# A batched 64x64 matmul: plain fp32 loads from GpSimd, and the cast to bf16 in one VectorE instruction

## The chip, the cores and the metric

The kernel runs on one core of a Trainium2 chip. The metric is the device time of one execution in microseconds (us); the time given for a kernel is the median of several executions. Engines are named as in the profile: PE is TensorE's matmul, PEld its weight load, DVE is VectorE, ACT is ScalarE, POOL is GpSimd and SP is SyncE, which here only issues transfers. Transfers can be issued from SP, ACT and POOL. All of them are carried out by the core's 16 DMA engines; in the profile the queue of POOL is q0, that of SP is q1 and that of ACT is q10.

## The reference

```python
a = randn(1024, 64, 64) as float32
b = randn(1024, 64, 64) as float32
out = matmul(a, b) as float32          # 1024 products of 64x64 by 64x64
```

Each of the three tensors has 16.78 MB (16 MiB).

## The kernel before

The batch is worked off in 16 tiles `t` of 64 matrices for `b` and the result, and in 8 tiles `s` of 128 matrices for `a`; tile `s` of `a` serves the tiles `t = 2s` and `t = 2s + 1`.

**Loading a.** A tile of `a` has 2 MiB and comes in four quarters `h` of 512 KiB. Each quarter is a 128-partition transfer with one contiguous row of 4 KB for each partition. For `s >= 1` (`load_a`, L69) POOL issues three quarters that are cast from fp32 to bf16 on the way, into `a_sb` (L73), and SP issues the fourth as plain fp32 into `a_raw` (L77). Both come from `a_pool`, which has three buffers of each. The first tile (`load_first_a`, L80) is loaded as plain fp32, two quarters from SP and two from ACT, into two buffers that are borrowed from the result pool `o_pool`, which has eight (L48).

**Loading b.** `load_b(t)` (L93) fetches 1 MiB of fp32 in pieces of 512 bytes, from SP for even `t` and from ACT for odd `t`, into one of three buffers. `cast(t)` (L144) turns it into bf16 on DVE, except the first tile, which ACT casts, and the last, which the two share (L149, L151).

**Regrouping and transposing a.** `regroup(s)` (L99) writes the quarters into `a_bf`, in which the four quarters lie side by side for each row `v`: one DVE copy of the three bf16 quarters (L108) and one DVE cast of the fp32 quarter (L111). For `s = 0` four casts do it, two on DVE and two on ACT (L105). `transpose(s, j)` reads pairs of bf16 as fp32 words and transposes them on PE (L120); ACT copies the result to `at_sb` (L123). `spread(t)` (L133) is four DVE copies that place the transposed words into a block-diagonal tile `at_bd`.

**Multiplying and storing.** `multiply(t)` runs 64 matmuls (L189) in two halves. The results are copied from PSUM into a result buffer `o_sb` (L177): eight copies of ACT for even tiles, six of ACT and two of DVE for odd ones, and a split into smaller ones for the last. `store(t)` (L166) writes the 1 MiB of a tile from POOL, one tile later than it was made (`HOLD = 2`); only the last two tiles are stored from SP and ACT, in pieces.

**The order.** The order of each engine's instructions and of each queue's transfers is that of the program, written out by hand:

```python
for t in range(n_t):
    ...
        spread(t + 1)
        cast(t + 1)
    ...
        load_b(t + B_AHEAD)
    ...
        load_a(s + 1 + A_AHEAD)
    ...
        transpose(s + 1, 1)
    multiply(t)
    ...
        regroup(s + 2)
    ...
        transpose(s + 2, 0)
        store(t - HOLD + 1)
```

The lines for `a` run once for each pair of tiles. An instruction waits for the semaphores of what it reads and of the buffer that it overwrites, and everything behind it on its engine waits with it; a transfer waits on the queue of the engine that issues it.

Of the kernel before, what the change touches and what calls it, by code (L numbers as in the profile page):

```python
# [8 lines left out]
fp32 = mybir.dt.float32  # L9
bf16 = mybir.dt.bfloat16  # L10
# [3 lines left out]
def kernel(  # L14
# [14 lines left out]
    nc = tc.nc  # L29
    B, M, K = a.shape  # L30
    _, _, N = b.shape
# [8 lines left out]
    a_v = a.rearrange("(s g h) (mp v) k -> s h g mp (v k)", h=4, g=32, v=16)  # L40
# [4 lines left out]
    a_pool = ctx.enter_context(tc.tile_pool(name="a_pool", bufs=A_AHEAD))  # L45
    b_pool = ctx.enter_context(tc.tile_pool(name="b_pool", bufs=B_AHEAD))
    work = ctx.enter_context(tc.tile_pool(name="work", bufs=2))
    o_pool = ctx.enter_context(tc.tile_pool(name="o_pool", bufs=8))  # L48
    t_psum = ctx.enter_context(
        tc.tile_pool(name="t_psum", bufs=4, space=bass.MemoryType.PSUM)  # L50
    )
# [9 lines left out]
    a_tiles, b_tiles, abf_tiles, at_tiles, bbf_tiles = {}, {}, {}, {}, {}  # L61
# [6 lines left out]

    def load_a(s):  # L69

        a_sb = a_pool.tile([128, 3, 16, 64], bf16, name="a_sb")
        for h in range(3):
            nc.gpsimd.dma_start(  # L73
                out=a_sb[:, h, :, :].rearrange("p v k -> p (v k)"), in_=a_v[s, h], single_packet=True
            )
        a_raw = a_pool.tile([128, 16, 64], fp32, name="a_raw")
        nc.sync.dma_start(out=a_raw[:].rearrange("p v k -> p (v k)"), in_=a_v[s, 3])  # L77
        a_tiles[s] = a_sb, a_raw

    def load_first_a():  # L80

        raw = [
            o_pool.tile([128, 8, 2, 2, 64], fp32, name="o_sb")[:].rearrange(
                "p gh j wl n -> p (gh j wl n)"
            )
            for _ in range(2)
        ]
        parts = [raw[h % 2][:, 1024 * (h // 2) : 1024 * (h // 2) + 1024] for h in range(4)]
        for h in range(4):
            (nc.scalar if h % 2 else nc.sync).dma_start(out=parts[h], in_=a_v[0, h])  # L90
        a_tiles[0] = parts

    def load_b(t):  # L93
        b_sb = b_pool.tile([128, 16, 128], fp32, name="b_sb")
        queue = nc.scalar if t % 2 else nc.sync
        queue.dma_start(out=b_sb[:], in_=b_v[t])  # L96
        b_tiles[t] = b_sb

    def regroup(s):  # L99
        a_sb = a_tiles.pop(s)  # L100
        a_bf = work.tile([128, 16, 4, 64], bf16, name="a_bf")
        if s == 0:
            for h in range(4):
                copy = nc.scalar.copy if h % 2 else nc.vector.tensor_copy
                copy(a_bf[:, :, h, :], a_sb[h].rearrange("p (v k) -> p v k", v=16))  # L105
        else:
            cast_sb, raw = a_sb
            nc.vector.tensor_copy(  # L108
                a_bf[:, :, 0:3, :], cast_sb[:].rearrange("p h v k -> p v h k")
            )  # L110
            nc.vector.tensor_copy(a_bf[:, :, 3, :], raw[:])  # L111
        abf_tiles[s] = a_bf
        at_tiles[s] = work.tile([128, 2, 32, 2, 4, 4], fp32, name="at_sb")

    def transpose(s, j):
        a_cols = abf_tiles[s][:].rearrange("p v h k -> p v (h k)").bitcast(fp32)
        for wl in range(2):
            at_ps = t_psum.tile([128, 4, 128], fp32, name="at_ps")
            for vo in range(4):
                nc.tensor.transpose(  # L120
                    at_ps[:, vo, :], a_cols[:, 4 * vo + 2 * j + wl, :], identity[:]
                )
            nc.scalar.copy(  # L123
                at_tiles[s][:, j, :, wl, :, :],
                at_ps[:].rearrange("p vo (g mp) -> p g mp vo", mp=4),
            )

    def spread(t):
        half = slice(16 * (t % 2), 16 * (t % 2) + 16)
        bd = bd_tiles[t % N_BD]  # L130
        for h in range(4):
            rows = slice(32 * h, 32 * h + 32)
            nc.vector.tensor_copy(  # L133
                bd[rows, :, :, :, h, :].rearrange("p j g wl mo -> p j (g wl) mo"),
                at_tiles[t // 2][rows, :, half, :, :, :].rearrange(
                    "p j g wl mp vo -> p j (g wl) (mp vo)"
                ),
            )

    def cast(t):  # L140
        b_bf = work.tile([128, 16, 128], bf16, name="b_bf")
        b_sb = b_tiles.pop(t)
        if t < n_t - 1:
            (nc.vector.tensor_copy if t else nc.scalar.copy)(b_bf[:], b_sb[:])  # L144
        else:
            for gq in range(4):
                rows = slice(4 * gq, 4 * gq + 4)
                if gq % 2:
                    nc.vector.tensor_copy(b_bf[:, rows, :], b_sb[:, rows, :])  # L149
                else:  # L150
                    nc.scalar.copy(b_bf[:, rows, :], b_sb[:, rows, :])  # L151
        bbf_tiles[t] = b_bf

    def store(t):
        for piece in held.pop(t):
            piece()
# [51 lines left out]
            held[t] = [lambda q=q: put(q, 8 if whole else 4) for q in ([0] if whole else [0, 4])]  # L208

    with tc.manual_schedule():  # L210
        load_first_a()

        nc.vector.memset(warm[:, 0:1], 0.0)
        nc.scalar.copy(warm[:, 1:2], warm[:, 0:1])  # L214
        load_b(0)
        load_b(1)
        nc.vector.memset(bd_tiles[0][:], 0.0)  # L217
        make_identity(nc, identity)
        nc.gpsimd.memset(bd_tiles[1][:, 0], 0.0)
        load_a(1)  # L220
        load_b(2)
        nc.gpsimd.memset(bd_tiles[1][:, 1], 0.0)
        load_a(2)
        regroup(0)
        transpose(0, 0)
        transpose(0, 1)
        spread(0)
        cast(0)
        for t in range(n_t):
            s, half = t // 2, t % 2  # L230
            if t + 1 < n_t:
                spread(t + 1)
                cast(t + 1)
            if t + B_AHEAD < n_t:
                load_b(t + B_AHEAD)
            if half == 0 and 0 < s < n_s - 1 - A_AHEAD:
                load_a(s + 1 + A_AHEAD)
            if half == 0 and 0 < s < n_s - 1:
                transpose(s + 1, 1)
            multiply(t)  # L240
            if t == 0:
                regroup(1)
                load_a(A_AHEAD)
                load_a(A_AHEAD + 1)
                transpose(1, 0)
                transpose(1, 1)
            elif t == 1:
                regroup(2)
            elif half == 0 and s + 2 < n_s:
                regroup(s + 2)  # L250
            if half == 1 and s + 2 < n_s:
                transpose(s + 2, 0)
            if t >= HOLD - 1:
                store(t - HOLD + 1)
        for t in range(n_t - HOLD + 1, n_t):
            store(t)
# [30 lines left out]
```

## Time and profile before

| | |
|---|---|
| runs | 134.62, 134.85, 134.93 us; median 134.85 |
| profiled execution, first to last instruction | span 133.4 us; the page gives no other time for this execution, so what lies around the span is 1.4 us measured against the median |
| busy: PE, PEld | 64.4 us (48%), 61.1 us (46%) |
| busy: DVE, ACT, POOL | 94.6 us (71%), 87.9 us (66%), 33.0 us (25%) |
| DMA engines | busy nine tenths or more in 38 of 40 slices of the span |
| bytes, by DMA queues | 45.01 MB |
| bytes, by HBM | 33.55 MB read, 16.78 MB written |
| loads of `a` on POOL | 21 of 256 KB as written, median 16.4 us from issue to landing |
| raw quarters of `a` on SP | 7 of 512 KB, median 18.7 us |
| stores on POOL | 14 of 1 MB, median 21.6 us |

A row of the groups of instructions gives the line, the engine, the operation, what it writes and reads, the shapes and the count; then the busy time of the group and the mean ns of one; then the engine's idle time just ahead of it and what ended most of that. In the rows of slices each digit is the busy share of a fortieth of the span in tenths, and 9 is 90% or more. The GB/s row and the queues count a transfer by the bytes that it writes. A DMA packet is the unit in which a queue hands work to one of the 16 engines; the trace has a record of each, with its size and duration.

### The profile page before, as it was taken

The numbers are of one execution on the slowest core, as the hardware profiler recorded it, in microseconds if no ns is written. First come the engines' busy times: TensorE is split into PE (matmuls) and PEld (weight loads), VectorE is DVE, ScalarE is ACT, GpSimd is POOL, SyncE is SP. The second block draws the span as 40 slices with busy tenths as digits, with TensorE's granted clock in tenths as the row PEclk, the third lists the DMA queues.
The fourth block names the chain that finished last, engine by engine and source line by source line (L and its number), as shares of the span: only waits on it lengthen the run. The fifth ranks groups of instructions, "written<-read, shape, count | busy, mean of one in ns | idle before, by whom it ended". The sixth has DMA issues, their size and how long they took to land.

```text
span 133.4 us, 2837 instructions
## 1 busy us (share of the span) xinstructions
PE 64.4 (48%) x1152; PEld 61.1 (46%) x1152; DVE 94.6 (71%) x120; ACT 87.9 (66%) x161; POOL 33.0 (25%) x43
## 2 busy tenths in 40 slices
PE   0006406960089384289518970956197363970000
PEld 0006306950089274189418950945196363960000
DVE  5930399109998809995999699959999995987000
ACT  3225424999036998969595969696968969099600
POOL 8991000420090070341233021203020410300000
PEclk9999975797557999856985699599959955599555
DMA  3999999999999999999999999999999999999990
GB/s 77 371 329 311 307 311 281 284 306 325 327 312 401 316 320 333 399 384 397 311 281 375 406 389 351 304 316 390 394 396 387 396 392 391 402 405 398 382 319 18
DMA packets 19021, 45.01 MB, mean 337 GB/s; under 512 B 1088, under 2 KB 3136, under 8 KB 19008
## 3 DMA queue, kind: packets, MB, share of 16 engines
q0 software_dynamic: 6832, 20.19, 50.1%
q1 hardware_dynamic: 7120, 14.68, 30.4%
q10 hardware_dynamic: 5056, 9.96, 19.7%
q8 instruction: 9, 0.15, 0.4%
q14 instruction: 4, 0.03, 0.1%
HBM read 33.55 MB, written 16.78 MB: 377 GB/s over the span
## 4 chain that ended last, share of the span: by engine, by line
DMA 53%; DVE 15%; ACT 13%; PE 6%; issue 5%; SPq 2%; DVEq 0%; ACTq 0%
DMA b_sb<-in_b_dram 53%; ACT o_sb L177 9%; DVE at_bd L133 6%; PE o_ps L189 4%; DVE b_bf L144 4%; DVE o_sb L177 3%; PE at_ps L120 2%; ACT at_sb L123 2%; ACT b_bf L144 1%; SPq L90 1%; DVE a_bf L108 1%; SPq L96 1%; ACT b_bf L151 1%; DVE a_bf L111 0%; SPq L77 0%
## 5 line engine op out<-in xcount | busy, mean ns | idle before, releaser
L177 ACT COPY o_sb<-o_ps 64x512 f32<-64x512 f32 x106 | 61.5, 580 | 10.3 <-PE o_ps L189 9.0
L189 PEld LDWEIGHTS <-at_bd 128*128 128x128 bf16 x1024 | 42.3, 113 | 39.5 <-DVE b_bf L144 25.7
L189 PE MATMUL o_ps<-b_bf,at_bd 128*128 128x64 bf16 x960 | 42.6, 216 | 35.4 <-DVE b_bf L144 23.4
L133 DVE COPY at_bd<-at_sb 32x1024 f32<-32x1024 f32 x64 | 46.9, 733 | 14.1 <-ACT at_sb L123 11.8
L120 PE MATMUL at_ps<-identity,a_bf 128*128 128x128 f32 x128 | 21.2, 335 | 19.4 <-ACT a_bf L105 11.2
L166 POOL DMA_DIRECT2D out_dram<-o_sb x14 | 15.4, 1097 | 56.9 <-ACT at_sb L123 23.4
L120 PEld LDWEIGHTS at_ps<-identity,a_bf 128*128 128x128 f32 x128 | 19.3, 180 | 19.5 <-issue 19.5
L123 ACT COPY at_sb<-at_ps 128x512 f32<-128x512 f32 x32 | 17.5, 590 | 11.0 <-PE at_ps L120 7.8
L144 DVE CAST b_bf<-b_sb 128x2048 bf16<-128x2048 f32 x14 | 17.8, 1271 | 9.6 <-DMA b_sb<-in_b_dram 9.4
L73 POOL DMA_DIRECT2D a_sb<-in_a_dram x21 | 13.6, 662 | 26.4 <-DVE a_bf L108 19.4
L177 DVE COPY o_sb<-o_ps 64x512 f32<-64x512 f32 x14 | 9.7, 690 | 0.3
L108 DVE COPY a_bf<-a_sb 128x3072 bf16<-128x3072 bf16 x7 | 6.7, 950 | 0.0
L105 ACT CAST a_bf<-o_sb 128x1024 bf16<-128x1024 f32 x2 | 2.1, 1044 | 5.2 <-DMA o_sb<-in_a_dram 5.2
L111 DVE CAST a_bf<-a_raw 128x1024 bf16<-128x1024 f32 x7 | 4.8, 683 | 0.0
L144 ACT CAST b_bf<-b_sb 128x2048 bf16<-128x2048 f32 x1 | 1.9, 1900 | 3.9 <-DMA b_sb<-in_b_dram 3.9
L105 DVE CAST a_bf<-o_sb 128x1024 bf16<-128x1024 f32 x2 | 2.8, 1382 | 1.9 <-DMA o_sb<-in_a_dram 1.9
L217 DVE MEMSET at_bd<- 128x4096 f32 x1 | 3.5, 3472 | 0.8 <-issue 0.8
L177 DVE COPY o_sb<-at_ps 64x256 f32<-64x256 f32 x8 | 3.4, 422 | 0.5 <-PE at_ps L189 0.4
L151 ACT CAST b_bf<-b_sb 128x512 bf16<-128x512 f32 x2 | 1.1, 615 | 3.6 <-DMA b_sb<-in_b_dram 3.6
L177 ACT COPY o_sb<-at_ps 64x256 f32<-64x256 f32 x8 | 2.9, 366 | 0.1
L214 ACT ACT_TABLE_LOAD x1 | 1.3, 1283 | 2.3 <-issue 2.3
L189 PE MATMUL at_ps<-b_bf,at_bd 128*128 128x64 bf16 x64 | 2.0, 193 | 1.0 <-DVE at_bd L133 1.0
(12 smaller groups left out, 6.1 us busy)
## 6 DMA issues: line engine op xcount, KB each, us to landing
out_dram<-o_sb POOLq DMA_DIRECT2D x14, 1024.0 KB, 21.6
a_sb<-in_a_dram POOLq DMA_DIRECT2D x21, 256.0 KB, 16.4
a_raw<-in_a_dram SPq DMA_DIRECT2D x7, 512.0 KB, 18.7
o_sb<-in_a_dram SPq DMA_DIRECT2D x2, 512.0 KB, 5.9
o_sb<-in_a_dram ACTq DMA_DIRECT2D x2, 512.0 KB, 7.1
out_dram<-o_sb SPq DMA_DIRECT2D x2, 512.0 KB, 7.5
out_dram<-o_sb SPq DMA_DIRECT2D x2, 256.0 KB, 7.8
out_dram<-o_sb ACTq DMA_DIRECT2D x2, 256.0 KB, 5.5
```

The source lines that it names most:

```text
L73: nc.gpsimd.dma_start(out=a_sb[:, h, :, :].rearrange("p v k -> p (v k)"), in_=a_v[s, h], single_packet=True)
L105: copy(a_bf[:, :, h, :], a_sb[h].rearrange("p (v k) -> p v k", v=16))
L108: nc.vector.tensor_copy(a_bf[:, :, 0:3, :], cast_sb[:].rearrange("p h v k -> p v h k"))
L111: nc.vector.tensor_copy(a_bf[:, :, 3, :], raw[:])
L120: nc.tensor.transpose(at_ps[:, vo, :], a_cols[:, 4 * vo + 2 * j + wl, :], identity[:])
L123: nc.scalar.copy(at_tiles[s][:, j, :, wl, :, :], at_ps[:].rearrange("p vo (g mp) -> p g mp vo", mp=4),)
L133: nc.vector.tensor_copy(bd[rows, :, :, :, h, :].rearrange("p j g wl mo -> p j (g wl) mo"), at_tiles[t // 2][rows, :, half, :, :, :].rearrange(
L144: (nc.vector.tensor_copy if t else nc.scalar.copy)(b_bf[:], b_sb[:])
L166: store_queue(t, lo).dma_start(out=o_v[t, :, lo : lo + n, :], in_=o_sb[:, lo : lo + n].rearrange("p gh j wl n -> p (gh j wl n)"),)
L177: copies[2 * par + wl](dst, src)
L189: nc.tensor.matmul(o_ps[:, gl, g % 2, j, :], at_bd[:, j, g, :, u], b_bf[:, g, 64 * u : 64 * u + 64], start=(u == 0), stop=(u == 1),)
L217: nc.vector.memset(bd_tiles[0][:], 0.0)
```

## The change

For `s >= 1` the three quarters that POOL loads are no longer cast on the way: all four quarters land as fp32 in one tile, `a_sb`, with the queues and the count of the transfers as before. `regroup` is then one DVE instruction that reads all four quarters and casts them while it writes `a_bf`. The first tile of `a` goes into a buffer of `a_pool` as well, still from SP and ACT, so that the pool's three buffers serve eight tiles instead of seven; `load_first_a` goes. The result pool has seven buffers instead of eight, and none is borrowed.

```diff
-    o_pool = ctx.enter_context(tc.tile_pool(name="o_pool", bufs=8))
+    o_pool = ctx.enter_context(tc.tile_pool(name="o_pool", bufs=7))
...
     def load_a(s):
 
-        a_sb = a_pool.tile([128, 3, 16, 64], bf16, name="a_sb")
-        for h in range(3):
-            nc.gpsimd.dma_start(
-                out=a_sb[:, h, :, :].rearrange("p v k -> p (v k)"), in_=a_v[s, h], single_packet=True
-            )
-        a_raw = a_pool.tile([128, 16, 64], fp32, name="a_raw")
-        nc.sync.dma_start(out=a_raw[:].rearrange("p v k -> p (v k)"), in_=a_v[s, 3])
-        a_tiles[s] = a_sb, a_raw
-
-    def load_first_a():
-
-        raw = [
-            o_pool.tile([128, 8, 2, 2, 64], fp32, name="o_sb")[:].rearrange(
-                "p gh j wl n -> p (gh j wl n)"
-            )
-            for _ in range(2)
-        ]
-        parts = [raw[h % 2][:, 1024 * (h // 2) : 1024 * (h // 2) + 1024] for h in range(4)]
+        a_sb = a_pool.tile([128, 4, 16, 64], fp32, name="a_sb")
         for h in range(4):
-            (nc.scalar if h % 2 else nc.sync).dma_start(out=parts[h], in_=a_v[0, h])
-        a_tiles[0] = parts
+            dst = a_sb[:, h, :, :].rearrange("p v k -> p (v k)")
+            if s == 0:
+                (nc.scalar if h % 2 else nc.sync).dma_start(out=dst, in_=a_v[s, h])
+            elif h < 3:
+                nc.gpsimd.dma_start(out=dst, in_=a_v[s, h], single_packet=True)
+            else:
+                nc.sync.dma_start(out=dst, in_=a_v[s, h])
+        a_tiles[s] = a_sb
...
-                copy(a_bf[:, :, h, :], a_sb[h].rearrange("p (v k) -> p v k", v=16))
+                copy(a_bf[:, :, h, :], a_sb[:, h, :, :])
         else:
-            cast_sb, raw = a_sb
-            nc.vector.tensor_copy(
-                a_bf[:, :, 0:3, :], cast_sb[:].rearrange("p h v k -> p v h k")
-            )
-            nc.vector.tensor_copy(a_bf[:, :, 3, :], raw[:])
+            nc.vector.tensor_copy(a_bf[:], a_sb[:].rearrange("p h v k -> p v h k"))
...
-        load_first_a()
+        load_a(0)
```

## The prediction

> **What bounds the kernel now.** I began with the page: the engine shares, the slices of the span, the DMA queues and the chain that ended last.
>
> ```profile
> PE 64.4 (48%) x1152; PEld 61.1 (46%) x1152; DVE 94.6 (71%) x120; ACT 87.9 (66%) x161; POOL 33.0 (25%) x43
> ...
> DMA  3999999999999999999999999999999999999990
> GB/s 77 371 329 311 307 311 281 284 306 325 327 312 401 316 320 333 399 384 397 311 281 375 406 389 351 304 316 390 394 396 387 396 392 391 402 405 398 382 319 18
> ...
> q0 software_dynamic: 6832, 20.19, 50.1%
> q1 hardware_dynamic: 7120, 14.68, 30.4%
> q10 hardware_dynamic: 5056, 9.96, 19.7%
> ...
> HBM read 33.55 MB, written 16.78 MB: 377 GB/s over the span
> ...
> DMA 53%; DVE 15%; ACT 13%; PE 6%; issue 5%; SPq 2%; DVEq 0%; ACTq 0%
> ```
>
> No compute engine is above 71%, but the DMA row is full in 38 of 40 slices. The rate in that row sags to 281 to 330 in the first two thirds and stands at 390 to 400 later. That sag is a matter of counting: the queues' sum is 45.01 MB, HBM's is 50.33 MB, and the difference is the 21 casting loads, which read 11.01 MB and are counted as the 5.51 MB they write. The windows show it (columns: us, busy time of the engines, TensorE clock, DMA share, GB/s):
>
> ```profile
> 3.00:90.00 87.00, 45.41 (x752) 43.16 (x752) 63.26 (x77) 59.27 (x106) 24.72 (x32) 0.80 1.06 336
> 90.00:125.00 35.00, 18.99 (x400) 17.93 (x400) 29.98 (x43) 27.17 (x52) 5.91 (x5) 0.79 1.03 394
> 125.00:132.00 7.00, 0.00 (x0) 0.00 (x0) 0.00 (x0) 0.79 (x3) 0.00 (x0) 0.50 0.73 258
> ```
>
> 3 to 90 us holds nearly all casting loads: 336 x 87 = 29.2 MB, plus the 5.5 MB not counted, is 34.7 MB, or 399 GB/s by the bytes read. 90 to 125 us, nearly without casts, runs at 394. So a cast byte costs the DMA engines about what any other byte costs, and the end is set by 50.33 MB through engines that are never empty. DMA shares over 1 mean that packets overlap by 3 to 6%.
>
> **The casting loads become plain loads** (21 transfers on POOL). They write 11.01 MB into SBUF instead of 5.51 MB and read the same 11.01 MB. What matters is engine time per 4 KB read: 2688 packets over 16 engines is 168 packets per engine, so each ns per packet is 0.168 us. The packet records give 172 ns for a cast packet. A plain 4 KB load packet has 176 ns on SP on average (162 in the windows after 60 us) and 167 on ACT; a 4 KB store packet on POOL 168. Because of the overlap I also counted the packets in service in each 5 us from 4 to 128 us and solved by least squares for the times that fill 16 engines: cast 158 +- 2 ns, plain load 162 +- 2, 2 KB of b 85 +- 1, 4 KB store 165 +- 1 (windows of 10 us: 153 and 162). Bounds: low, late plain packets against cast packets as recorded, (162 - 172) x 0.168 = -1.7 us; high, a plain load that costs two b packets, (170 - 158) x 0.168 = +2.0 us. I take the fit, as it alone removes the overlap: (162 - 158) x 0.168 = **+0.7 us**. Nothing hides this term, since DMA is the bound.
>
> **The regroup becomes one DVE cast.** The rows now:
>
> ```profile
> L144 DVE CAST b_bf<-b_sb 128x2048 bf16<-128x2048 f32 x14 | 17.8, 1271 | 9.6 <-DMA b_sb<-in_b_dram 9.4
> ...
> L177 DVE COPY o_sb<-o_ps 64x512 f32<-64x512 f32 x14 | 9.7, 690 | 0.3
> L108 DVE COPY a_bf<-a_sb 128x3072 bf16<-128x3072 bf16 x7 | 6.7, 950 | 0.0
> ...
> L111 DVE CAST a_bf<-a_raw 128x1024 bf16<-128x1024 f32 x7 | 4.8, 683 | 0.0
> ```
>
> The two old instructions take 1.47 us from start to the next one's start (96.02 to 97.49 in the timeline). For 4096 fp32 elements: 2048 take 1.23 us (the undisturbed cast of b), 1024 take 0.68, so 0.53 ns an element, and 1.23 + 2048 x 0.53 ns = 2.31 us. Bounds: 1.2 us at the rate of L108, 4.4 us at the one-element rate of the evacuations from PSUM (422 ns for 256, 690 for 512: 1.05 ns an element). I take 2.31, from the two rows of the same fp32 to bf16 cast: +0.8 us each, 5.6 us of DVE in all. Its cover is DVE's waits for loads of b:
>
> ```profile
> 63.35 1.23 DVE L144 CAST b_bf<-b_sb 128x2048 bf16<-128x2048 f32 x1 [1.55 <-DMA b_sb<-in_b_dram]
> ...
> 76.15 1.23 DVE L144 CAST b_bf<-b_sb 128x2048 bf16<-128x2048 f32 x1 [1.07 <-DMA b_sb<-in_b_dram]
> ...
> 89.08 1.23 DVE L144 CAST b_bf<-b_sb 128x2048 bf16<-128x2048 f32 x1 [1.31 <-DMA b_sb<-in_b_dram]
> ```
>
> Each follows one regroup and takes its 0.8 us with 0.3 to 0.75 to spare. The regroups at 35.5 and 41.3 us come before waits of 0.57 and 3.98 us. The last, at 96.0, has no wait close behind, but the transposes it feeds start at 99.29, behind multiply(11), and it would end at 98.3; the last load of b is issued on ACT's queue at 102.03 behind evacuations. Only the regroup at 35.5 shows at once: PE starts its transposes at 37.24 on it, so load_b(6) (41.93) goes out 0.8 us later, still behind a raw quarter that lands at 53.4. If the cover is gone, the end has slack: after 125.85, when the last store is issued, DMA still needs 5.6 us, and 258 x 7 = 1.8 MB move after 125 us against 0.5 MB in the last two stores. 1.3 MB at 394 GB/s is 3.3 us by which compute may be late. I charge **0**.
>
> One sign speaks against the longer cast: DVE's first fp32 cast of a quarter (5.08 us) took 2.07 us beside POOL's 1.85 us memset, the other 0.69. The Trainium skill ("SBUF — State Buffer", Who interferes with whom) says that a VectorE copy or cast in a two-port mode and GpSimd lock each other out for a whole instruction, and names descriptor generation as what starves. By that rule a POOL issue could wait one cast, an estimate of 2.3 us. Whether it does or not, queue 0 holds earlier work: POOL's loads land 8.0 to 29.2 us after issue, median 16.4. Charge 0.
>
> **Waits moved.** Buffers of a are now freed by the whole cast, not by its two parts. On POOL the loads for s=4 (23.57) and s=5 (36.79) wait about 1.4 us longer, the store of tile 1 (39.23) behind them; queue 0 still has loads landing until 32.9 and a store until 46.2. On SP the raw quarters wait 0.8 us longer, with load_b(4) and load_b(6) behind them, which land 25 and 21 us after issue. load_a(3) now needs buffer 0, free after regroup(0) at 11.1 us; its issues move from 8.3 to 11.2, behind loads that land until 23.9. The cast also needs all four quarters at its start: the tightest, for s=2, lands at 35.32 against a start at 35.53. All 0, while DMA stays full.
>
> **Seven result buffers.** Tile t now waits for the store of t-7. First writes against landings in the trace: tile 12 at 103.73 against store 5 at 96.32 is the closest, 7.4 us. 0; if stores land over 7 us later, ACT's evacuations wait. The first a leaves the result pool, with the same queues and quarters: 0.
>
> **Sum.** Against the profiled execution (span 133.4, which is 1.4 us under the median of the runs): 133.4 + 0.7 = 134.1. On the median 134.85 that is 135.5.
>
> **The rivals.** (1) Plain packets are the cheaper ones: they need no conversion, and cast packets have the same 172 ns in every window, while plain ones fall to 159 to 162 where DMA is otherwise the same. Against: the fit, and 399 against 394 GB/s. It decides from 1.6 ns a packet below the cast (0.27 us); its end is -1.7 us, 133.2. This ends faster. (2) A byte read costs the same either way, as 399 and 394 suggest: 134.85. (3) DVE loses its double rate on the four-quarter pattern: 4.4 us, 3.0 more per regroup. With about 1.1 us of cover in each of four pairs, and 4.5 for the first two: 4 x 1.9 + 1.5 = 9.1, less 3.3 of slack, +5.8: 140.6. Against: L108 reads the same pattern at a fast rate. (4) The plain loads are cut otherwise than the stores' 4 KB packets and cost the +2.0 bound, or lateness of DVE outgrows the slack by as much: 136.9.
>
> **How the numbers follow.** Forecast (+0.3 to +1.5) 0.45; rival 1 0.27; rival 2 0.17; rival 3 0.05; rival 4 0.06. Measurement of this kernel tells about 0.2%, 0.27 us. Faster 0.27, same 0.17, slower 0.56. The range 133.5 to 136.9 leaves out rival 3, the far end of rival 1 and some of rival 4; the forecast's own is 135.1 to 136.4.
>
> **What would show it.** The queues' sum rises from 45.0 to 50.5 MB, and the GB/s row stands near 395 from the second slice on with the DMA row still full: right. Packets of the plain loads at 162 to 166 ns by the same fit: the term. One DVE row of seven casts at 2.3 us, with the waits for b reduced by 0.8: the cover. A cast at 4.4 us, nines that vanish from the DMA row, or ACT waiting for a landing store would prove it wrong.

## The result: 7.2 us slower, and the profile after

The changed kernel takes 142.07 us at the median (141.87 to 142.25, 4 runs) against 134.89 for the kernel before in the same comparison (134.62 to 135.33, 4 runs). The ratio is 1.0524, with a 95% interval from 1.0502 to 1.0547. The profiled execution of the changed kernel took 142.25 us with a span of 140.4. The forecast of 135.5 missed, and so did its range, which ended at 136.9. Ratios in this document leave out executions more than 1.5% above the fastest of the same kernel, which concerns two of the four with the plain quarters on SP.

The page of the changed kernel, with the engines' shares, the slices, queue 0, HBM and the chain that ended last:

```profile
PE 67.7 (48%) x1152; PEld 64.5 (46%) x1152; DVE 99.7 (71%) x113; ACT 88.2 (63%) x161; POOL 35.0 (25%) x43
...
DMA  3999999999999999999999999999999999999990
GB/s 80 385 391 336 331 348 392 356 338 366 373 388 393 384 347 369 373 385 394 394 354 349 396 394 396 358 342 366 395 396 387 396 394 397 389 406 406 380 332 31
...
q0 software_dynamic: 6832, 25.69, 48.1%
...
HBM read 33.55 MB, written 16.78 MB: 358 GB/s over the span
...
DMA 61%; DVE 14%; SPq 7%; ACT 6%; issue 4%; PE 3%; DVEq 0%; ACTq 0%
```

The DMA row is as full as before: 38 nines, so the engines are hardly ever without work. But now no load is cast, every byte is counted once, and the GB/s row still does not stand at 395 throughout. It drops to 331 to 358 in several slices of the first two thirds, and there the drop is real. Windows, with the columns of the windows before (us, engines, TensorE clock, DMA share, GB/s):

```profile
3.00:100.00 97.00, 50.09 (x806) 48.06 (x807) 70.70 (x76) 61.43 (x111) 27.05 (x33) 0.79 1.03 370
100.00:132.00 32.00, 17.62 (x351) 16.49 (x348) 27.66 (x37) 25.09 (x48) 5.51 (x5) 0.77 1.03 395
132.00:139.00 7.00, 0.00 (x0) 0.00 (x0) 0.00 (x0) 1.00 (x3) 0.00 (x0) 0.50 0.74 260
```

The later stretch (395 against 394 before) and the tail (260 against 258) have not changed. The whole loss is in the stretch that holds the loads of a: 370 x 97 = 35.9 MB, which at the 399 GB/s of before would have taken 90.0 us. That is 7.0 us of the 7.0 by which the spans differ.

Inside that stretch the loss is not even. The page's slice at 10.5 to 14.0 us shows 336 while only loads run, and the slices with many stores, or with little `b` among the loads (the one at 21.1 to 24.6 us), show 390 and more. The same window of both kernels, first before, then after:

```profile
12.00:21.00 9.00, 2.80 (x14) 2.55 (x13) 5.33 (x8) 4.06 (x5) 0.00 (x0) 0.84 1.08 309
```

```profile
12.00:21.00 9.00, 3.33 (x16) 3.19 (x17) 4.79 (x8) 2.34 (x4) 1.60 (x3) 0.86 1.04 339
```

No store runs in it. Before, 309 GB/s are written into SBUF, and by the packet records of the same window 403 are read, 189 of them by casts. After, 339 are written and 339 are read. By the same records a packet of `b` (2 KB, four pieces of 512 bytes) takes 89 ns in this window before and 113 after.

DVE did as predicted: the cast took 2338 ns, and DVE still waits for loads of b.

```profile
L129 DVE CAST b_bf<-b_sb 128x2048 bf16<-128x2048 f32 x14 | 17.4, 1245 | 10.7 <-DMA b_sb<-in_b_dram 10.5
...
L96 DVE CAST a_bf<-a_sb 128x4096 bf16<-128x4096 f32 x7 | 16.4, 2338 | 1.1 <-DMA a_sb<-in_a_dram 1.1
```

### The profile page after: what moved, and what is told of

Its sections match the earlier page's. It is cut to its first block, busy times and chain, and to the rows that moved or that the text cites. A ratio compares the mean times of both kernels' runs of the same rounds, so it can differ in the third digit from the quotient of the medians.

```text
span 140.4 us, 2845 instructions
## 1 busy us (share of the span) xinstructions
PE 67.7 (48%) x1152; PEld 64.5 (46%) x1152; DVE 99.7 (71%) x113; ACT 88.2 (63%) x161; POOL 35.0 (25%) x43
## 4 chain that ended last, share of the span: by engine, by line
DMA 61%; DVE 14%; SPq 7%; ACT 6%; issue 4%; PE 3%; DVEq 0%; ACTq 0%
DMA b_sb<-in_b_dram 41%; DMA a_sb<-in_a_dram 20%; DVE at_bd L118 6%; ACT o_sb L162 5%; SPq L79 5%; DVE a_bf L96 3%; DVE b_bf L129 3%; PE at_ps L105 3%; DVE o_sb L162 2%; SPq L85 2%; SPq L75 1%; ACT b_bf L136 0%; ACT at_sb L108 0%; DVEq L96 0%; DVEq L129 0%
## 5 line engine op out<-in xcount | busy, mean ns | idle before, releaser
L174 PEld LDWEIGHTS <-at_bd 128*128 128x128 bf16 x1024 | 44.1, 115 | 41.2 <-DVE b_bf L129 27.3
L174 PE MATMUL o_ps<-b_bf,at_bd 128*128 128x64 bf16 x960 | 44.3, 220 | 37.2 <-DVE b_bf L129 25.3
L151 POOL DMA_DIRECT2D out_dram<-o_sb x14 | 18.7, 1335 | 57.5 <-ACT at_sb L108 24.6
L105 PE MATMUL at_ps<-identity,a_bf 128*128 128x128 f32 x128 | 22.7, 352 | 21.4 <-ACT a_bf L94 11.9
L105 PEld LDWEIGHTS at_ps<-identity,a_bf 128*128 128x128 f32 x128 | 20.9, 191 | 21.6 <-issue 21.4
L129 DVE CAST b_bf<-b_sb 128x2048 bf16<-128x2048 f32 x14 | 17.4, 1245 | 10.7 <-DMA b_sb<-in_b_dram 10.5
L77 POOL DMA_DIRECT2D a_sb<-in_a_dram x21 | 12.2, 589 | 31.0 <-DVE a_bf L96 23.1
L96 DVE CAST a_bf<-a_sb 128x4096 bf16<-128x4096 f32 x7 | 16.4, 2338 | 1.1 <-DMA a_sb<-in_a_dram 1.1
L94 ACT CAST a_bf<-a_sb 128x1024 bf16<-128x1024 f32 x2 | 2.1, 1044 | 5.9 <-DMA a_sb<-in_a_dram 5.9
L85 ACT MOVE_SHAPE b_sb<-in_b_dram x8 | 0.5, 64 | 6.5 <-DVE b_bf L129 6.5
L94 DVE CAST a_bf<-a_sb 128x1024 bf16<-128x1024 f32 x2 | 2.6, 1316 | 2.3 <-DMA a_sb<-in_a_dram 2.3
```

The costliest lines, as they stand in the source:

```text
L77: nc.gpsimd.dma_start(out=dst, in_=a_v[s, h], single_packet=True)
L94: copy(a_bf[:, :, h, :], a_sb[:, h, :, :])
L96: nc.vector.tensor_copy(a_bf[:], a_sb[:].rearrange("p h v k -> p v h k"))
L105: nc.tensor.transpose(at_ps[:, vo, :], a_cols[:, 4 * vo + 2 * j + wl, :], identity[:])
L151: store_queue(t, lo).dma_start(out=o_v[t, :, lo : lo + n, :], in_=o_sb[:, lo : lo + n].rearrange("p gh j wl n -> p (gh j wl n)"),)
L174: nc.tensor.matmul(o_ps[:, gl, g % 2, j, :], at_bd[:, j, g, :, u], b_bf[:, g, 64 * u : 64 * u + 64], start=(u == 0), stop=(u == 1),)
```

## The experiments

Three theories stood at the start. **W**: writing plain quarters of `a` and the small pieces of `b` into SBUF together is slow. **Q**: plain loads on POOL's queue are slow in themselves. **C**: compute, by DVE's longer regroup or the lost result buffer, holds the transfers back.

### Seven result buffers alone

```diff
-    o_pool = ctx.enter_context(tc.tile_pool(name="o_pool", bufs=8))
+    o_pool = ctx.enter_context(tc.tile_pool(name="o_pool", bufs=7))
```

> The kernel before, with seven result buffers in place of eight, and nothing else. Three theories of the 7 us. W (writes): the DMA engines are slower while plain quarters of a and the 512-byte pieces of b are both written into SBUF and no store runs beside them. Q (queue): plain loads issued from POOL are slow in themselves. C (compute): DVE's longer regroup or the lost result buffer makes the loads and stores come later. W and Q expect 134.9, no change within 0.3 us, as the closest reuse of a result buffer has 7.4 us to spare. C, if the buffer is the cause, expects 138 to 142.

Measured: 134.91 us (10 runs) against 134.80, ratio 1.0011 (0.9995 to 1.0027). The buffer costs nothing that can be measured.

### A longer regroup alone

```diff
             nc.vector.tensor_copy(a_bf[:, :, 3, :], raw[:])
+            nc.vector.tensor_copy(pad_out[:], pad_in[:])
```

> The kernel before, its loads untouched, with one more DVE cast of 1280 fp32 elements (about 0.83 us) after each of the seven regroups, which makes a regroup as long as the changed kernel's. W: DVE's waits for b take it up, 134.5 to 135.6. C: 138 to 142.

Measured: 134.91 us (10 runs) against 135.01, ratio 0.9992 (0.9976 to 1.0008). The groups of its profile show where the time went: the added cast came out at 923 ns, and DVE's idle time before the cast of b fell from 9.6 us to 5.7.

```profile
L147 DVE CAST b_bf<-b_sb 128x2048 bf16<-128x2048 f32 x14 | 17.2, 1227 | 5.7 <-DMA b_sb<-in_b_dram 5.5
...
L114 DVE CAST pad_out<-pad_in 128x1280 bf16<-128x1280 f32 x7 | 6.5, 923 | 0.0
```

With these two runs C is out.

### The plain quarters on SP

```diff
-                nc.gpsimd.dma_start(out=dst, in_=a_v[s, h], single_packet=True)
+                nc.sync.dma_start(out=dst, in_=a_v[s, h])
```

> The changed kernel with the 21 plain quarters of a issued from SP instead of POOL; the bytes, the rows and DVE's work are the same. W expects 141 to 144, since the same bytes are written into SBUF. Q expects 134 to 137, since no load is left on POOL. C expects about 142.

Measured: ratio 1.0959 (1.0905 to 1.1012), about 147.7 us by it. Q expected 134 to 137 and falls. W's 141 to 144 was too low as well. Two windows of its profile, of an execution of 149.68 us:

```profile
20.00:30.00 10.00, 6.36 (x104) 6.09 (x101) 5.51 (x6) 8.24 (x15) 1.02 (x1) 0.81 1.04 326
...
128.00:146.00 18.00, 8.34 (x163) 7.81 (x160) 11.03 (x19) 12.08 (x24) 1.47 (x2) 0.69 0.73 250
```

In the first, nearly all traffic is loads, none of them from POOL, and the rate is 326 GB/s: W's loss on the other queues. In the second the DMA engines are no longer full: in the DMA row two slices between 129 and 137 us stand at 6 and 2. This is a second loss. A possible reading is that `b` comes later with four quarters of `a` ahead of each even tile on SP (load_b(6) landed at 72.2 us instead of 68.2), so that at the end stores alone are left and cannot fill the engines. That reading was not tested.

### The rates alone

> No product at all: ten stages of transfers alone, one after the other, each closed by a DVE copy that waits for all of it. Rates by the bytes read, in the middle of a stage. W: b alone 280 to 300 GB/s; plain a alone about 405 on POOL and on SP with ACT; plain a beside b 330 to 350, on POOL as on SP; casting a beside b about 400; stores beside b about 390; stores beside plain a about 400. Q: plain a alone on POOL and plain a on POOL beside b below 350, all else 390 or more, b alone and plain a on SP beside b among them. C: all of them 385 or more.

The windows below lie in these stages, in this order: b alone on SP and ACT; plain a alone on POOL; plain a alone on SP and ACT; plain a on POOL beside b; casting a on POOL beside b; and stores on POOL beside plain a on SP and ACT. There is no matmul, so the columns are us, busy DVE, ACT and POOL, the clock, DMA share and GB/s.

```profile
30.00:44.00 14.00, 0.00 (x0) 0.00 (x0) 0.00 (x0) 1.00 1.06 290
52.00:64.00 12.00, 0.00 (x0) 0.00 (x0) 1.59 (x3) 1.00 1.03 414
72.00:82.00 10.00, 0.00 (x0) 0.00 (x0) 0.00 (x0) 1.00 1.03 413
92.00:108.00 16.00, 0.00 (x0) 0.00 (x0) 0.00 (x0) 1.00 1.04 337
...
146.00:161.00 15.00, 0.00 (x0) 0.00 (x0) 0.00 (x0) 1.00 1.08 305
...
200.00:210.00 10.00, 0.00 (x0) 0.00 (x0) 3.72 (x5) 1.00 1.02 419
```

The first four are W's numbers: b alone 290, plain a alone 414 and 413 on whatever queue, the two together 337. That is what the two get if they take turns, each at its own rate: by the packet records a runs at 160 and b at 176, and 160/414 + 176/290 = 0.99 of the time. So the pieces of b are slow by themselves, and beside plain loads they cost what they cost alone. The fifth counts casts by what they write; by the packet records b runs at 208 and the casts read 193, together 401, and write 96. By the bytes read, turns would fill 208/290 + 193/414 = 1.18 of the time, by the bytes written 208/290 + 96/414 = 0.95. A cast takes from b about the turns that half its bytes need. Plain a on SP beside b on ACT gave 358 (118 to 128 us) with more a than b in it. The stage of stores beside b did not come apart from its neighbours and is repeated below. These stages, and those of the two later runs of transfers alone, were executed once; where they repeat each other they agree (b alone 290 and 290, plain a beside b 337 and 338).

### The pieces of b taken away

```diff
+    b_f = b.rearrange("(t q) (w k) n -> t (q w) (k n)", q=64, w=2)
...
-        queue.dma_start(out=b_sb[:], in_=b_v[t])
+        queue.dma_start(out=b_sb[:].rearrange("p g n -> p (g n)"), in_=b_f[t])
```

Each of the 128 partitions now gets one row of 8 KB. The same edit in the changed kernel and in the kernel before:

> The changed kernel, but each tile of b is read as 128 rows of 8 KB instead of 2048 pieces of 512 bytes: the same bytes in another order, so the products are of other rows of b. W expects 132 to 136, and plain loads beside b at about 400 GB/s. Q and C expect 140 to 142.

> The kernel before with b read as rows of 8 KB, as e3_flat_after is of the changed one; the products are of other rows of b. W: writing 512-byte pieces into SBUF is what is slow, and casts beside them relieve it; without the pieces nothing is left to relieve, so 131.5 to 133.5, within 1.2 us of e3_flat_after at 132.2. If instead plain loads on POOL (Q) or DVE's work (C) cost 7 us whatever b does, 123 to 127.

Measured: 132.16 us for the changed kernel (ratio 0.9818 to the kernel before as it is, 0.9775 to 0.9861), and 132.88 for the kernel before (0.9844, 0.9809 to 0.9880). With its pieces, b makes the plain loads 7.2 us dearer than the casts; without them, the difference is gone, and both are some 2 us faster than the kernel before. In the stretch that ran at 339 GB/s the changed kernel now reaches 414:

```profile
12.00:21.00 9.00, 5.45 (x53) 5.05 (x54) 4.66 (x7) 4.17 (x6) 1.60 (x3) 1.00 1.02 414
```

### The width written, or the conversion?

A casting load differs from a plain one in two ways: it writes half as much, and it goes through a conversion. In one kernel all four quarters are converted by POOL's loads to int32, in its partner to bf16.

```diff
-        a_sb = a_pool.tile([128, 4, 16, 64], fp32, name="a_sb")
+        a_sb = a_pool.tile([128, 4, 16, 64], mybir.dt.int32 if s else fp32, name="a_sb")
...
-                nc.sync.dma_start(out=dst, in_=a_v[s, h])
+                nc.gpsimd.dma_start(out=dst, in_=a_v[s, h], single_packet=True)
```

> The changed kernel with all four quarters of a on POOL, each converted on the way from fp32 to int32, so that a casting load writes the full 4 bytes an element; DVE casts int32 to bf16 (a is rounded to whole numbers). W: the bytes written into SBUF decide, so it is as slow as the changed kernel, 140 to 146. A further rival, P: not the width but the conversion in the DMA engines' path relieves b; then 133 to 137, like the kernel before.

> The kernel before with all four quarters of a cast to bf16 by POOL's loads and one bf16 copy on DVE: the partner of e7_cast32 with half the width written. W: 133.5 to 136, as the bytes read, about 400 GB/s, already bound the kernel before beside its casts. P: the same. C: below 134.5, as DVE's regroup falls by 0.3 us.

Measured: int32 143.34 us, ratio 1.0619 (1.0592 to 1.0646); bf16 135.15, ratio 1.0004 (0.9988 to 1.0019). The two kernels differ in the regroup and in the result buffers too, which the first two experiments showed to cost nothing. P falls: for `a`, what relieves b is that the neighbour writes 2 bytes an element instead of 4. Window 12 to 21 us of the int32 kernel, whose rate is that of the changed kernel:

```profile
12.00:21.00 9.00, 3.43 (x16) 3.13 (x16) 4.73 (x7) 2.34 (x4) 1.76 (x3) 0.90 1.09 337
```

The bf16 kernel also tells that a fourth casting quarter brings nothing more.

### One and two quarters cast

```diff
+    CAST = 1
...
-        a_sb = a_pool.tile([128, 3, 16, 64], bf16, name="a_sb")
+        a_sb = a_pool.tile([128, CAST, 16, 64], bf16, name="a_sb")
+        a_raw = a_pool.tile([128, 4 - CAST, 16, 64], fp32, name="a_raw")
```

The kernel with two quarters cast has `CAST = 2`. Both have seven result buffers.

> The kernel before with two of POOL's three quarters cast on the way and one plain, seven result buffers. W, in numbers: loads go at the slower of a reading side of about 400 GB/s (e5_stages, casts beside b) and a writing side on which b's pieces take 1/290 and a's written bytes 1/414 (e5_stages, each alone). For 52% b and 48% a that is 339 GB/s with no cast (337 measured), 356 with one quarter of four cast, 375 with two, 397 with three. Scaled to the 7.2 us of the changed kernel: 2.5 us for two, so 136.5 to 138.4. If any plain load on POOL cost the whole: 141 to 143.

> The same with one of POOL's three quarters cast. By the two sides of e9_two_cast: 4.8 us, so 138.7 to 140.6. If the loss is the same for any plain load on POOL: 141 to 143; if it comes only when no quarter is cast: 134 to 136.

Measured: 136.29 us with two, ratio 1.0134 (1.0109 to 1.0158), and 138.91 with one, 1.0331 (1.0304 to 1.0357). On 134.50 that is +1.8 and +4.4 us, beside 0 with three and +7.2 with none. The two sides had given +2.5 and +4.8; two casts came out 0.2 us under the expected range, so the sides are a fair but not an exact account.

### Bytes or pieces?

> No product: seven stages of loads alone. What makes b slow, its bytes written or its count of pieces? If the written bytes of a piece (W as it stands): b plain on POOL 280 to 300 GB/s, cast to bf16 380 or more by bytes read, converted to int32 280 to 300, b cast beside plain a about 400. If each piece has its own price whatever its width: 280 to 300 for all three of b. In pieces of 1 KB and 2 KB on SP and ACT, a price a piece gives 350 and 380 (half and a quarter of the extra 0.53 ns per 512 bytes and engine group over 414), and in pieces of 512 bytes 290 again.

Stages, by windows: b plain on POOL; b cast to bf16 on POOL; b converted to int32 on POOL; b in pieces of 1 KB, of 2 KB and of 512 bytes on SP and ACT.

```profile
41.00:55.00 14.00, 0.00 (x0) 0.00 (x0) 0.00 (x0) 1.00 1.02 289
64.00:71.00 7.00, 0.00 (x0) 0.00 (x0) 0.00 (x0) 1.00 1.83 182
80.00:87.00 7.00, 0.00 (x0) 0.00 (x0) 0.00 (x0) 1.00 1.85 359
...
120.00:133.00 13.00, 0.00 (x0) 0.00 (x0) 0.00 (x0) 1.00 1.10 350
141.00:154.00 13.00, 0.00 (x0) 0.00 (x0) 0.00 (x0) 1.00 1.03 382
166.00:179.00 13.00, 0.00 (x0) 0.00 (x0) 0.00 (x0) 1.00 1.06 290
```

A price for each piece fits the plain stages. With 16 engines, 512 bytes at 290 GB/s take 28.2 ns, 1 KB at 350 takes 46.8, 2 KB at 382 takes 85.8, and the 4 KB rows of a at 414 take 158. As an estimate from these rates, that is about 9.7 ns a piece and 18.5 ns for each 512 bytes; it comes out 2 ns short for 2 KB. The converting stages fit neither theory, and W's 380 or more for bf16 and 280 to 300 for int32 both missed. By bytes read, bf16 runs at 364 and int32 at 359, so b converted at full width is much faster than b plain. The records show why the comparison is not clean: a converting load sends each piece as a packet of its own (42 ns, two in flight by the DMA share of 1.85), where the plain one sends eight pieces in a packet of 231 ns. The stage of b cast beside plain a did not mix as meant: b ran at 25 GB/s until a was done.

The Trainium skill ("DMA: Bandwidth & Descriptors", Specifications) gives 512 bytes as the smallest transfer for line rate. Here 512-byte pieces into SBUF run at 290 GB/s and 4 KB rows at 414, so the measurement decides otherwise.

### Which side

> No product: six stages of transfers alone, on which side the pieces of b are slow. Totals by bytes moved. If it is the writing into SBUF (W): b beside plain a 337 as in e5_stages, b beside a converted to int32 330 to 345, b beside rows of 4 KB moved from SBUF to SBUF 300 to 350 although these read nothing from HBM, b beside stores 385 or more. If it is the reading from HBM: b beside SBUF-to-SBUF rows 385 or more, as b beside stores. Stores alone 390 to 405, as at the end of both kernels.

In this order: b beside plain a; b beside a converted to int32; b beside rows of 4 KB moved from SBUF to SBUF; b beside stores; stores alone.

```profile
45.00:60.00 15.00, 0.00 (x0) 0.00 (x0) 0.00 (x0) 1.00 1.04 338
72.00:87.00 15.00, 0.00 (x0) 0.00 (x0) 0.00 (x0) 1.00 1.10 337
102.00:114.00 12.00, 0.00 (x0) 0.00 (x0) 0.00 (x0) 1.00 1.04 337
...
140.00:156.00 16.00, 0.00 (x0) 0.00 (x0) 0.00 (x0) 1.00 1.03 395
165.00:171.00 6.00, 0.00 (x0) 0.00 (x0) 0.00 (x0) 1.00 1.00 337
```

The neighbour in the third stage reads nothing from HBM and slows the total to 337 all the same; the neighbour in the fourth writes nothing into SBUF and the total is 395. Nor does each packet simply take its own time in its engine, whatever it does: the 177 GB/s of b and 218 of stores in the fourth (packet records) would fill 177/290 + 218/402 = 1.15 of the time in turns, with the 402 that stores alone reach in the kernel before (117 to 121 us). The limit lies on the side that writes into SBUF. The last line missed: stores alone were to run at 390 to 405, as at the end of both kernels, and ran at 337 here, and at 332 in the last stage of the rates alone, though from the queue that reached 402 in the kernel before. Why is open.

## Why the prediction was wrong

- **What bounds the kernel.** Right: the DMA engines were full before and are full after, and nothing but their rate moved the end.
- **The step that failed** is the term "The casting loads become plain loads", put at +0.7 us with bounds of -1.7 and +2.0. It measured +7.2 (7.0 in the span). The mechanism behind the number was wrong, not only its size. The prediction gave each kind of packet one price and asked what a plain packet of `a` costs. That price barely moved: in the changed kernel POOL's plain load packets take 175 ns on average, against 172 for the casts. What rose was the price of the 8192 packets of `b`, from 88 to 96 ns on average and to 113 in the window from 12 to 21 us, where no store runs and packets overlapped less (a DMA share of 1.04 instead of 1.08). 113 ns is also what a packet of `b` takes alone: 2 KB over 16 engines at 290 GB/s. Casts and stores had hidden a part of that price, and the change took the casts away.
- **Why the fit could not see it.** In the kernel before, plain loads and pieces of `b` nearly always run beside casts or stores. A fit over such windows has no row of the state that the change creates. The same fit over the packet records of the changed kernel (4 to 134 us) gives 168 ns for a plain load, 100 for a packet of `b` and 149 for a store, where it had given 162, 85 and 165.
- **What in the profile could have warned.** The GB/s row of before, in slices without stores, is the rate written into SBUF. With `b` in the mix it was 281 to 329; the 371 of the second slice was 4 KB rows of `a` without any `b`. The change asks for some 400 there, and no row showed that this can be had. The 394 GB/s of 90 to 125 us did not show it, since more than half of that traffic was stores. "A cast byte costs the DMA engines about what any other byte costs" was read as a property of casts; it was a property of the mix.
- **The regroup** at 2.31 us: measured 2.338. Charged 0, and the lengthened regroup alone changes nothing. The lock between DVE and GpSimd that the prediction allowed for did not matter for the end either: POOL's stores took 1335 ns to issue instead of 1097, whether by that lock or not, and the DMA row stayed full.
- **Waits moved, and seven buffers**: charged 0; the buffers were shown by a run of their own, the waits only by the DMA row that stays full.
- **The rivals.** Rival 4 had the nearest place, plain loads dearer than expected, but bounded it by the trace's own prices, at 136.9. Rival 3's 140.6 is nearer in number alone: it needed a cast of 4.4 us, and the cast took 2.3. Rivals 1 and 2 did not come.

## What to carry to other kernels

In this kernel full DMA engines set the time, a transfer had a price on two sides, and what a cast saved was on the side that writes into SBUF. Before a change raises the bytes written there, look for a stretch of the trace that already writes at the rate the change needs, with the same sizes of pieces beside it; a price per packet fitted in another mix does not carry over. Small contiguous pieces are where to look first. Here rows of 8 KB in place of 512 bytes for `b` made casts and plain loads alike, though the layout of this product does not allow that edit as it stands.

## What the runs showed of the hardware

- Plain loads into SBUF by size of piece: 290 GB/s at 512 bytes, 350 at 1 KB, 382 at 2 KB, 414 at 4 KB.
- 512-byte pieces beside plain 4 KB rows into SBUF: 337 GB/s in all, whether the rows come from HBM or from SBUF, which is what the two rates of their own give in turns; beside casts of 4 KB rows to bf16 401 by bytes read; beside stores 395.
- A casting load of 512-byte pieces runs at 364 GB/s by bytes read, faster than the plain one at 289, and an int32 conversion at 359. Beside large packets of other queues it got 25 GB/s.
- Open: why a piece has its price on the writing side, why conversion lifts it, and why stores alone ran at 337 in a stage of their own and near 400 at the end of the kernels.
